# Hybrid decoder trunk on one core: order of the gate normalisations, of a weight cast and of the residual's instructions

## The chip, the cores and the metric

The kernel runs on one core of one Trainium2 chip. The metric is the device time of one execution in microseconds (us). A core has five instruction queues: TensorE (PE), VectorE (DVE), ScalarE (ACT), GpSimd (POOL) and SyncE (SP, which here only starts DMAs). Each engine carries out its own instructions in the order in which they stand; the engines wait for each other by semaphores.

## The reference

Two layers over a sequence of 512 tokens of width 1024, in float32. Cut to what matters here:

```python
n = rmsnorm(h, attn_norm[l])
u, v_sgu, q, k, v_att = split(n @ w_in[l])
u, v_sgu = gelu(u), gelu(v_sgu)
vg = rmsnorm over groups of 128 (v_sgu)              # the "gate values"
y_sgu = u * (tril(w_s) @ vg + b_s)                   # per chunk of 128 tokens
q, k = partial_rope(q), partial_rope(k)
p = softmax(mask(q k^T / 8))                         # 4 heads, two maps each
y_att = rmsnorm((p[0] - lam * p[1]) @ v_att) * (1 - lambda_init)
h = h + concat(y_sgu, y_att) @ w_out[l]
h = h + conv_ffn(rmsnorm(h, ffn_norm[l]))            # gated, causal width 3
```

A last rmsnorm follows the two layers.

## The kernel before, in words

`h` lies transposed in eight SBUF tiles `hT[m]` of 128 features x 512 tokens. Every float32 operand of a product is split into a high part (a cast to float32r) and a low part (what is left), and a product is three matmuls: high x high, high x low, low x high.

**Weights.** `specs` lists blocks of 128x1024 in the order of use; `block(j)` (line 158) starts block j's DMA into `raw`, casts it to `wh` on ACT and subtracts into `wl` on DVE or POOL. There are three buffers each of `raw`, `wh` and `wl`, so a cast waits until PE has done with an older block. In each layer blocks 0 to 19 are `w_in`, 20 to 27 `w_out`, then `w_up` and `w_down`. `AHEAD` says how many blocks past the one in use are prepared; a cast stands in ACT's queue at the place where `block` was called.

**Order.** `pin` chains all instructions of an engine in the order of the code, so the order of the Python calls is the order of each queue (the small rsqrt steps on DVE, lines 378 to 383, alone are free). `run(steps, n)` takes n steps of a generator of projections; after each step one entry of the queue `due` is called: it holds the small work on DVE, ACT and POOL that follows a projection.

**Mixer, layer 0.** `both_first` projects the first half of the gate values (`vs_0`) together with the first queries; then come `vs_1`, the first keys (`k_0`, `k_1`) and the first values (`va`). `gate_values` (line 542) turns a half of gate values into `vg`: gelu and square on ACT, sums, rsqrt and a product on DVE, and `split` (cast on ACT, low part on DVE). `rope` (line 488) turns queries or keys: shuffle and product on DVE, product and sum on POOL, then `split`. The scores are 16 units (4 heads x 4 query tiles, `Unit`): `scores` on PE into two banks, `mn` (mask and minimum) on DVE, `exps` on ACT, `difference` on DVE, the transpose `turn` on PE, `high` and `low`, then `values` on PE. Between these stand up to three steps of the next projections. `spatial` (line 479) masks and splits the 128x128 mixing weights `wsp`.

**Output projection.** `project` fills the banks of output tiles 0 to 3 during the scores; `late` holds tiles 4 and 5; tiles 6 and 7 come last, with blocks 26 and 27. `residual` (line 913) adds a bank to `hT[m]` on DVE, and `norm.feed(m)` makes `gh_f` (ACT), `gl_f` (DVE), the square (ACT) and its sum `acc_f` (POOL). The feed forward part starts with the matmuls `g<-gh_f`.

In the views a helper at line 119 records nearly all instructions, so tiles are read by name; `L119` is no place in the kernel. The number behind a `wh` or `raw` in an order is a buffer's, not a block's.

Of the kernel before, what the change touches and what calls it, by code (L numbers as in the profile page):

```python
# [21 lines left out]
P = 128  # L22
# [4 lines left out]
DEPTH = 2  # L27
# [42 lines left out]
def trunk(ctx: ExitStack, tc, a, out):  # L70
# [16 lines left out]
    def fslot(name):  # L87
        return sp.tile([P, S], F32, tag="s", name=name)
# [53 lines left out]
    specs = []  # L142
# [11 lines left out]
    AHEAD = [2]  # L154

    def block(i):
        while len(loaded) <= min(i + AHEAD[0], len(specs) - 1):
            j = len(loaded)
            n = specs[j].shape[-1]
            if j >= len(specs) - 6:  # L160
                loaded.append(kept(j, n))
                continue
            raw = wp.tile([P, 1024], F32, tag="raw", name=f"raw{j}")[:, :n]
            h = wp.tile([P, 1024], F32R, tag="wh", name=f"wh{j}")[:, :n]
            lo = wp.tile([P, 1024], F32R, tag="wl", name=f"wl{j}")[:, :n]
            (sync if j < 6 else nc.sync).dma_start(out=raw, in_=specs[j])
            act.copy(h, raw)
            mixer = j % (len(specs) // DEPTH) < 28
            eng = gps if (j > 6 if mixer else j % 3 == 1) else dve
            eng.tensor_sub(lo, raw, h.bitcast(F32))  # L170
            loaded.append((h, lo))
        return loaded[i]
# [48 lines left out]
    nxt = [0]  # L221
# [30 lines left out]
    def tok_gemm(banks, xs):  # L252

        for k, x in enumerate(xs):
            if k % 4 == 0:
                h, lo = next_block()
            c = slice(k % 4 * 256, (k % 4 + 1) * 256)
            tok_step(banks, x, (h[:, c], lo[:, c]), k == 0, k == len(xs) - 1)
            yield
# [104 lines left out]
    def rotary_turn():  # L364
        for nm, wide, dst in wides:
            bank = tr_bank(f"rot{nm}")
            for t in range(NT):
                transpose(bank[:, t * P : (t + 1) * P], wide[:, t * P : (t + 1) * P], ident)
            dve.tensor_copy(dst, bank)

    SHUF = [(i + HALF if i < HALF else i - HALF if i < ROT else i) for i in range(32)]

# [58 lines left out]
    def split(name, src, eng=None):  # L431
        h, lo = slot(f"{name}h"), slot(f"{name}l")
        act.copy(h, src)
        (eng or dve).tensor_sub(lo, src, h.bitcast(F32))
        return h, lo
# [10 lines left out]
    for l in range(DEPTH):  # L446
# [28 lines left out]
        def spatial():  # L475
            gps.affine_select(
                out=wsp, in_=wsp, compare_op=ALU.is_ge, fill=0.0, base=0,
                pattern=[[0, NG], [1, P]], channel_multiplier=-1,
            )
            act.copy(ws_h, wsp)  # L480
            gps.tensor_sub(ws_l, wsp, ws_h.bitcast(F32))
# [6 lines left out]
        def rope(banks, store, at, name):  # L488

            t1, sh = [None, None], [None, None]  # L490

            def turn(j):
                sh[j] = tmp(f"{name}{l}_{at + j}sh")
                dve.stream_shuffle(sh[j], banks[j], SHUF)
                t1[j] = tmp(f"{name}{l}_{at + j}t1")
                dve.tensor_mul(t1[j], banks[j], Cr)
                gps.tensor_mul(sh[j], sh[j], Sr)
                gps.tensor_add(t1[j], t1[j], sh[j])

            def part(j):  # L500
                store[at + j] = split(f"{name}{l}_{at + j}", t1[j])

            due.extend([partial(turn, 0), partial(turn, 1), partial(part, 0), partial(part, 1)])

        def query_banks(hp):
            return [mm_bank(f"q{2 * hp + j}_{l}") for j in range(2)]
# [1 line left out]
        def queries(hp):  # L508
            banks = query_banks(hp)
            yield from feat_gemm(banks, xs)  # L510
            rope(banks, qs, 2 * hp, "q")

        def keys(hp):
            banks = [mm_bank(f"k{2 * hp + j}_{l}") for j in range(2)]
            yield from feat_gemm(banks, xs)
            rope(banks, ks, 2 * hp, "k")

        def values(hp):
            banks = [mm_bank(f"va{b}_{hp}_{l}") for b in range(2)]
# [19 lines left out]

        vg, us, ya, ys = [None] * 2, [None] * NG, [None] * NH, [None] * NG  # L540

        def gate_values(gp, banks, steps):

            yield from steps
            gs = sm.tile([P, 8], F32, tag="gs", name=f"gs{l}_{gp}", bufs=2)
            vts, sqs = [None] * 2, [None] * 2
            r = []

            def gelu(b):
                vts[b] = tmp(f"vs{l}_{gp}_{b}")  # L550
                for x in range(2):
                    c = slice(x * 256, x * 256 + 256)
                    t = 2 * b + x
                    act.activation(vts[b][:, c], banks[b][:, c], AF.Gelu_apprx_tanh, scale=norm.rcol[:, t : t + 1])

            def square(b):
                sqs[b] = tmp(f"vq{l}_{gp}_{b}")
                act.activation(sqs[b], vts[b], AF.Square)

            def sums():  # L560
                for b in range(2):
                    dve.reduce_sum(
                        gs[:, 4 * b : 4 * b + 4], sqs[b].rearrange("p (x d) -> p x d", d=P), axis=mybir.AxisListType.X
                    )
                nc.vector.tensor_scalar(gs, gs, 1.0 / P, EPS, op0=ALU.mult, op1=ALU.add)
                r.append(rsqrt(gs, 8, f"gr{l}_{gp}"))

            def normed(b):
                v3 = vts[b].rearrange("p (x d) -> p x d", d=P)
                rb = r[0][:, 4 * b : 4 * b + 4].unsqueeze(2).to_broadcast([P, 4, P])  # L570
                dve.tensor_tensor(out=v3, in0=v3, in1=rb, op=ALU.mult)

            def parts():
                vg[gp] = [split(f"vg{l}_{gp}_{b}", vts[b]) for b in range(2)]

            due.extend([
                partial(gelu, 0), partial(gelu, 1), lambda: (square(0), square(1)), sums, nothing, nothing,
                lambda: (normed(0), normed(1)), parts,
            ])

        def gates(c):

# [154 lines left out]
        def value_banks(gp, bank=mm_bank):  # L737
            return [bank(f"vs{b}_{gp}_{l}") for b in range(2)]

        def both_first():  # L740

            vb, qb = value_banks(0), query_banks(0)

            def steps():
                for k, x in enumerate(xs):
                    tok_step(vb, x, first[0][k], k == 0, k == KD - 1)
                    yield
                    feat_step(qb, x, first[1][k], 0, k == 0, k == KD - 1)
                    yield

            yield from gate_values(0, vb, steps())
            rope(qb, qs, 0, "q")

        def products():
            if l == 0:
                yield from both_first()
                banks = value_banks(1, sc_bank)
            else:
                banks = value_banks(0)
                yield from gate_values(0, banks, tok_gemm(banks, xs))  # L760
                yield from queries(0)
                banks = value_banks(1)
            yield from gate_values(1, banks, tok_gemm(banks, xs))
            yield from keys(0)
            yield from values(0)
            yield from queries(1)
            yield from keys(1)
            yield from values(1)
            yield from gates(0)
            yield from gates(1)  # L770
            yield from project()
# [21 lines left out]
        steps = products()  # L793
        if l == 0:
            run(steps, 16)
            due.extend([nothing] * 4)
            norm.sums()
            for _ in rotary:
                pass
            run(steps, 4)  # L800
            norm.rows()
            run(steps, 2)
            rotary_turn()
        else:
            run(steps, 8)
            due.extend([nothing, nothing])
            run(steps, 2)
            norm.sums()
            run(steps, 3)
            norm.rows()  # L810
            run(steps, 2)
        Cr, Sr = fslot(f"Cr{l}"), fslot(f"Sr{l}")
        dve.tensor_mul(Cr, CT, norm.rstd)
        dve.tensor_mul(Sr, ST, norm.rstd)
        run(steps, 28 - (22 if l == 0 else 15))
        spatial()
        run(steps, 12)
        flush()
        nlam, sgain = small()
# [8 lines left out]
        for i in range(len(todo) + 2):  # L828
# [44 lines left out]
                u2.values()  # L873
            if i in MIX_AT:
                biased.append(mix(MIX_AT.index(i)))
            if i < 8:
                run(steps, 1)
            if i == len(todo):
# [31 lines left out]

        norm = Norm(f"f{l}", C_FN + l * KD)

        def residual(c, banks):
            for j in range(2):
                m = 2 * c + j
                dve.tensor_add(hT[m], banks[j], hT[m])
                norm.feed(m)

        for c in range(2):
            residual(c, pairs[c])  # L920
        run(more)
        residual(2, late)
        banks = [mm_bank(f"wo{6 + j}_{l}") for j in range(2)]
        run(feat_gemm(banks, mixed))
        residual(3, banks)
        pinned[0] = False


# [225 lines left out]
```

## Time and profile before

| | |
|---|---|
| time, median of 3 runs | 1164.84 us (1164.15 to 1165.5) |
| the profiled execution | 1166.31 us, its span 1164.6 us |
| PE busy | 1123.8 us, 96% of the span |
| DVE, ACT, POOL busy | 675.9, 478.3, 395.0 us |
| mean granted PE clock | 0.984 of full speed |
| DMA | 105.24 MB, mean 90 GB/s |

A row of a timeline begins with the start (us from the span's start) and the duration; then engine, line, operation, output<-inputs and shapes; in brackets the idle time of that engine just before, and what released it. A matmul's duration is longer than the step to the next one, since matmuls are pipelined: the step is read from the starts. [...]

### The profile page before, as it was taken

To read this page: it belongs to the slowest core of one execution; us is meant where nothing else is said; L and a number is where in the kernel's file an instruction comes from. 1 tells how busy PE (TensorE), PEld (TensorE's weight loads), DVE (VectorE), ACT (ScalarE), POOL (GpSimd) and SP (SyncE) were. 2 spreads that over 40 slices of the span, in tenths; PEclk is the share of its full clock that TensorE was granted. 3 is DMA by queue.
4 is the path that set the end of the run, shared out by engine and by line. 5 is a ranking of instruction groups with operands and counts; after the bars stand their busy time and mean duration, and the time that the engine had idled before them with its cause. 6 is when DMAs were issued, how large, how long until landed. Compare 5 with 4: busy or idle time off the path is not lost.

```text
span 1164.6 us, 14820 instructions
## 1 busy us (share of the span) xinstructions
PE 1123.8 (96%) x5637; PEld 941.4 (81%) x5637; DVE 675.9 (58%) x1267; ACT 478.3 (41%) x808; POOL 395.0 (34%) x305
## 2 busy tenths in 40 slices
PE   9959999799999999999999999979999999999996
PEld 7957888688888888888899788868888888888886
DVE  6667875475664225764347687735765622565634
ACT  6344453443443224443343554544444412344351
POOL 0446323522241113233456652251333211231351
PEclk9979999899999999999999999989999999999998
DMA  8212112222323223332332211213332232333222
GB/s 265 73 54 73 55 61 76 72 91 92 107 91 108 91 92 95 102 85 88 103 119 75 89 57 54 73 41 114 100 103 96 91 108 92 91 94 105 75 89 73
DMA packets 34215, 105.24 MB, mean 90 GB/s; under 512 B 4064, under 2 KB 8544, under 8 KB 34144
## 3 DMA queue, kind: packets, MB, share of 16 engines
q1 hardware_dynamic: 33712, 104.27, 28.5%
q8 instruction: 44, 0.72, 0.3%
q14 instruction: 27, 0.22, 0.1%
q10 hardware_dynamic: 432, 0.03, 0.0%
HBM read 102.19 MB, written 2.10 MB: 90 GB/s over the span
## 4 chain that ended last, share of the span: by engine, by line
PE 83%; DVE 6%; POOL 4%; ACT 3%; issue 3%; DVEq 0%; POOLq 0%; ACTq 0%
PE g L119 21%; PE v L119 21%; PE dn L119 18%; PE wo L119 6%; PE u L119 4%; PE q L119 3%; PE vs L119 3%; PE dl L119 2%; PE sc L119 1%; POOL wl L119 1%; PE av L119 1%; PE mx L119 1%; ACT wh L119 1%; DVE s L119 1%; DVE hT L119 1%
## 5 line engine op out<-in xcount | busy, mean ns | idle before, releaser
L119 POOL TENSOR_TENSOR wl<-raw,wh 128x1024 fp32r<-128x1024 f32 (+1 forms) x98 | 235.0, 2400 | 584.3 <-ACT wh L119 574.5
L119 ACT CAST wh<-raw 128x1024 fp32r<-128x1024 f32 (+1 forms) x192 | 194.0, 1016 | 373.2 <-issue 189.2
L119 DVE TENSOR_TENSOR wl<-raw,wh 128x1024 fp32r<-128x1024 f32 (+1 forms) x94 | 120.2, 1279 | 129.4 <-ACT wh L119 129.2
L119 PE MATMUL g<-gh_f,wh 128*128 128x512 f32 x352 | 137.1, 390 | 0.0
L119 PE MATMUL v<-gh_f,wh 128*128 128x512 f32 x352 | 137.1, 390 | 0.0
L119 PE MATMUL g<-gh_f,wl 128*128 128x512 f32 x352 | 137.0, 389 | 0.0
L119 PE MATMUL v<-gh_f,wl 128*128 128x512 f32 x352 | 136.9, 389 | 0.0
L119 PE MATMUL g<-gl_f,wh 128*128 128x512 f32 x352 | 136.9, 389 | 0.0
L119 PE MATMUL v<-gl_f,wh 128*128 128x512 f32 x352 | 136.9, 389 | 0.0
L119 DVE SCALAR_TENSOR_TENSOR cv<-up_cv,par,cv 128x512 f32<-128x512 f32 x88 | 74.3, 891 | 7.7 <-ACT cv L119 7.4
L119 PEld LDWEIGHTS g<-gh_f,wl 128*128 128x128 f32 x352 | 66.1, 188 | 13.8
L119 PEld LDWEIGHTS v<-gh_f,wl 128*128 128x128 f32 x352 | 66.1, 188 | 13.7
L119 PEld LDWEIGHTS v<-gh_f,wh 128*128 128x128 f32 x352 | 66.1, 188 | 13.6
L119 PEld LDWEIGHTS g<-gl_f,wh 128*128 128x128 f32 x352 | 66.1, 188 | 13.6
L119 PEld LDWEIGHTS v<-gl_f,wh 128*128 128x128 f32 x352 | 66.1, 188 | 13.6
L119 PEld LDWEIGHTS g<-gh_f,wh 128*128 128x128 f32 x352 | 66.1, 188 | 13.6
L119 DVE SCALAR_TENSOR_TENSOR cg<-up_cg,par,cg 128x512 f32<-128x512 f32 x88 | 71.1, 856 | 6.8 <-ACT cg L119 6.3
L119 DVE TENSOR_TENSOR up_cv<-v,rstd_f 128x512 f32<-128x512 f32 x44 | 30.2, 693 | 67.2 <-PE v L119 67.2
L119 DVE TENSOR_TENSOR up_cg<-g,rstd_f 128x512 f32<-128x512 f32 x44 | 30.0, 692 | 53.7 <-PE g L119 53.4
L119 ACT ACTIVATE s<-s,mn 128x128 f32<-128x128 f32 (+3 forms) x64 | 35.5, 557 | 61.1 <-DVE mn L119 61.1
L119 ACT ACTIVATE cg<-cg 128x512 f32<-128x512 f32 x44 | 27.8, 631 | 46.6 <-DVE cg L119 46.6
L119 DVE TENSOR_TENSOR hT<-dn,hT 128x512 f32<-128x512 f32 x28 | 19.1, 691 | 47.7 <-PE dn L119 47.7
(586 smaller groups left out, 2615.3 us busy)
## 6 DMA issues: line engine op xcount, KB each, us to landing
raw<-in_w_up SPq DMA_DIRECT2D x88, 512.0 KB, 3.4
raw<-in_w_dn SPq DMA_DIRECT2D x40, 512.0 KB, 3.5
raw<-in_w_in SPq DMA_DIRECT2D x36, 512.0 KB, 3.5
raw<-in_w_out SPq DMA_DIRECT2D x16, 512.0 KB, 3.5
hT<-in_xT SPq DMA_DIRECT2D x8, 256.0 KB, 4.7
or<-in_w_in SPq DMA_DIRECT2D x16, 128.0 KB, 4.5
raw<-in_w_dn SPq DMA_DIRECT2D x8, 256.0 KB, 3.4
out<-y SPq DMA_DIRECT2D x8, 256.0 KB, 2.2
```

The costliest lines, as they stand in the source:

```text
L119: return lambda *args, **kw: pin(getattr(self.engine, op)(*args, **kw))
```

## The change

Five edits. (1) In layer 0 the queries' turn is put ahead of the first half's normalisation, and of the second half of gate values only the gelu stays there: squares, sums, rsqrt, products and splits go to a queue `later`, from which each score unit takes two entries; `spatial` is the last of them. (2) In layer 0 the rotary factors `cr` and `sr` are made from the transposed bank directly, and the copies CT and ST (for layer 1) go to ACT. (3) Block 27 (the last of `w_out`) is prepared by a call ahead of the first residual, block 28 after the fourth; `AHEAD` is 0 between. (4) Block 27's low part goes from POOL to DVE. (5) `residual` takes all banks of a group, and each tile's add stands ahead of the `feed` of the tile before it. In layer 1 only (3), (4) and (5) move anything.

```diff
-            mixer = j % (len(specs) // DEPTH) < 28
-            eng = gps if (j > 6 if mixer else j % 3 == 1) else dve
+            i_l = j % (len(specs) // DEPTH)
+            eng = gps if (j > 6 and i_l != 27 if i_l < 28 else j % 3 == 1) else dve
...
-            dve.tensor_copy(dst, bank)
+            turned = fslot(f"{nm}r0")
+            dve.tensor_mul(turned, bank, norm.rstd)
+            act.copy(dst, bank)
+            yield turned
...
+            return [partial(f, b) for f in (gelu, square, sums) for b in range(2)] + [root] + [
+                partial(f, b) for f in (normed, part) for b in range(2)
+            ]
...
-            yield from gate_values(0, vb, steps())
-            rope(qb, qs, 0, "q")
+            yield from steps()
+            g, q = gate_work(0, vb), rope(qb, qs, 0, "q")
+            due.extend([nothing] * 4 + g[:2] + q[:2] + g[2:4] + [lambda: [f() for f in g[4:7]]] + q[2:] + g[7:])
+
+        later = deque()
...
+                yield from tok_gemm(banks, xs)
+                g = gate_work(1, banks)
+                due.extend(g[:2])
+                later.extend(g[2:])
...
-        spatial()
+        if l == 0:
+            later.append(spatial)
+        else:
+            spatial()
...
+            for _ in range(min(2, len(later))):
+                later.popleft()()
             if i < 8:
                 run(steps, 1)
...
-        def residual(c, banks):
-            for j in range(2):
-                m = 2 * c + j
-                dve.tensor_add(hT[m], banks[j], hT[m])
-                norm.feed(m)
-
-        for c in range(2):
-            residual(c, pairs[c])
+        def residual(m0, banks):
+            for m, b in enumerate(banks, m0):
+                dve.tensor_add(hT[m], b, hT[m])
+                if m > m0:
+                    norm.feed(m - 1)
+            norm.feed(m)
+
+        AHEAD[0] = 0
+        block(nxt[0] + 1)
+        residual(0, pairs[0] + pairs[1])
         run(more)
-        residual(2, late)
+        block(nxt[0] + 2)
+        AHEAD[0] = 2
+        residual(4, late)
         banks = [mm_bank(f"wo{6 + j}_{l}") for j in range(2)]
         run(feat_gemm(banks, mixed))
-        residual(3, banks)
+        residual(6, banks)
```

PE's own order is the same in both kernels. ACT at layer 0's residual, before, from the last attention output (`yah`) on:

```order
L119 ACTIVATE yah_3_3_2279<-ot_3_3_2274,sgain_935 128x512
L119 ACTIVATE gh_f_2315<-hT_85,par 128x512
L119 ACTIVATE acc_f_2313<-hT_85 128x512
L119 ACTIVATE gh_f_2321<-hT_86,par 128x512
L119 ACTIVATE sq_f_2325<-hT_86 128x512
...
L119 ACTIVATE gh_f_2359<-hT_90,par 128x512
L119 ACTIVATE sq_f_2363<-hT_90 128x512
L119 CAST wh_2369<-raw_2368 128x1024
L119 CAST wh_2375<-raw_2374 128x1024
L119 CAST wh_2405<-raw_2404 128x1024
```

And there now (`hT_85` to `hT_92` are tiles 0 to 7):

```order
L119 ACTIVATE yah_3_3_2279<-ot_3_3_2274,sgain_902 128x512
L119 CAST wh_2315<-raw_2314 128x1024
L119 ACTIVATE gh_f_2322<-hT_85,par 128x512
L119 ACTIVATE acc_f_2313<-hT_85 128x512
...
L119 ACTIVATE gh_f_2343<-hT_88,par 128x512
L119 ACTIVATE sq_f_2347<-hT_88 128x512
L119 CAST wh_2357<-raw_2356 128x1024
L119 ACTIVATE gh_f_2364<-hT_89,par 128x512
```

Block 27's cast has moved from behind six residual tiles to ahead of the first, block 28's from behind six to behind four.

DVE in layer 0 ahead of the first keys' turn (`gr`, `vs_1`, `vg_1` are the second half of gate values), before:

```order
L383 SCALAR_TENSOR_TENSOR gr_1_830<-gr_1t,gr_1_830 128x8
L119 TENSOR_TENSOR vs_1_0_781<-vs_1_0_781,gr_1_830 128x512
L119 TENSOR_TENSOR vs_1_1_796<-vs_1_1_796,gr_1_830 128x512
L119 TENSOR_TENSOR vg_1_0l<-vs_1_0_781,vg_1_0h 128x512
L119 TENSOR_TENSOR vg_1_1l<-vs_1_1_796,vg_1_1h 128x512
L119 STREAM_SHUFFLE k_0sh<-k_0_666 128x512
L119 TENSOR_TENSOR k_0t_909<-k_0_666,Cr_617 128x512
```

And there now:

```order
L119 TENSOR_TENSOR q_1l<-q_1t_653,q_1h 128x512
L119 TENSOR_TENSOR vs_0_0_587<-vs_0_0_587,gr_0_691 128x512
L119 TENSOR_TENSOR vs_0_1_602<-vs_0_1_602,gr_0_691 128x512
L119 TENSOR_TENSOR vg_0_0l<-vs_0_0_587,vg_0_0h 128x512
L119 TENSOR_TENSOR vg_0_1l<-vs_0_1_602,vg_0_1h 128x512
L119 STREAM_SHUFFLE k_0sh<-k_0_658 128x512
L119 TENSOR_TENSOR k_0t_822<-k_0_658,cr_610 128x512
```

What stands right ahead of the keys is now the first half; the second half has gone behind them.

DVE in score units 2 and 3 of layer 0 (`s_0_2`, `s_0_3` are the maps of head 0, `aTl` the low part of a transposed map), before:

```order
L119 SCALAR_TENSOR_TENSOR s_0_2_0_1051<-s_0_2_1_1052,cf_0_2_1075,s_0_2_0_1051 128x384
L119 TENSOR_TENSOR aTl_0_1_1073<-at_0_1_1061,aTh_0_1_1072 128x256
L119 STREAM_SHUFFLE q_2sh<-q_0_953 128x512
L119 TENSOR_TENSOR q_2t_1099<-q_0_953,Cr_617 128x512
L119 TENSOR_REDUCE o_0_937<-av_0_0_1080 128x128
L119 ISA s_0_3_0_1113,mn_0_3_1112<-sc_0_3_0_1104,mask 128x512
```

And there now:

```order
L386 SCALAR_TENSOR_TENSOR gr_1_1057<-gr_1t,gr_1_1057 128x8
L681 RECIPROCAL cf_0_2_1048<-esum_0_905 128x1
L682 SCALAR_TENSOR_TENSOR cf_0_2_1048<-esum_0_905,cf_0_2_1048,nlam_899 128x1
L119 SCALAR_TENSOR_TENSOR s_0_2_0_1024<-s_0_2_1_1025,cf_0_2_1048,s_0_2_0_1024 128x384
L119 TENSOR_TENSOR aTl_0_1_1046<-at_0_1_1034,aTh_0_1_1045 128x256
L119 TENSOR_TENSOR vs_1_0_790<-vs_1_0_790,gr_1_1057 128x512
L119 STREAM_SHUFFLE q_2sh<-q_0_920 128x512
L119 TENSOR_TENSOR q_2t_1087<-q_0_920,cr_610 128x512
L119 TENSOR_REDUCE o_0_904<-av_0_0_1053 128x128
L119 ISA s_0_3_0_1101,mn_0_3_1100<-sc_0_3_0_1092,mask 128x512
```

The second half's rsqrt steps and its products now stand between the units' instructions.

## Rows read from the trace of the kernel before

**Rows 1.** The page: busy us (share) by engine; DVE's low parts (busy, mean ns).

```profile
PE 1123.8 (96%) x5637; PEld 941.4 (81%) x5637; DVE 675.9 (58%) x1267; ACT 478.3 (41%) x808; POOL 395.0 (34%) x305
...
L119 DVE TENSOR_TENSOR wl<-raw,wh 128x1024 fp32r<-128x1024 f32 (+1 forms) x94 | 120.2, 1279 | 129.4 <-ACT wh L119 129.2
```

**Rows 2.** PE's waits: who waited for whom, total us, times, longest.

```profile
PE sc L119 <- ACT k_0h L119: 11.1, 1, 11.1
PE wo L119 <- ACT wh L119: 9.8, 2, 4.9
```

**Rows 3.** Busy time by stretch: PE, PEld, DVE, ACT, POOL (instructions), PEclk, DMA, GB/s.

```profile
64.57:75.62 11.05, 0.00 (x1) 0.01 (x2) 9.01 (x22) 1.84 (x3) 5.49 (x4) 0.69 0.27 92
77.30:82.20 4.90, 4.90 (x13) 3.80 (x12) 2.49 (x12) 4.33 (x9) 1.72 (x2) 0.50 0.00 2
84.00:107.00 23.00, 22.76 (x121) 17.20 (x120) 16.49 (x46) 10.86 (x29) 12.61 (x7) 1.00 0.23 69
90.00:160.00 70.00, 68.68 (x442) 57.33 (x443) 55.48 (x171) 34.52 (x100) 30.00 (x16) 1.00 0.19 61
```

**Rows 4.** PE's timeline around layer 0's first scores.

```profile
52.67 0.39 PE L119 MATMUL k<-gh_a,wl 128*128 128x512 f32 x1
...
75.62 0.47 PE L119 MATMUL sc<-k_0h,q_0h 64*128 64x128 f32 x2 [11.05 <-ACT k_0h L119]
...
83.97 0.39 PE L119 MATMUL sc<-k_0h,q_0h 64*128 64x256 f32 x2
...
88.99 0.44 PE L119 MATMUL sc<-k_0h,q_0h 64*128 64x384 f32 x2
...
102.94 0.66 PE L119 MATMUL at<-ident,s 128*128 128x128 f32 x4 [0.24 <-DVE aTl L119]
```

**Rows 5.** PE's timeline at the output projection's end, layers 0 and 1.

```profile
203.37 0.39 PE L119 MATMUL wo<-yah,wl 128*128 128x512 f32 x1
...
204.73 0.39 PE L119 MATMUL wo<-yah,wl 128*128 128x512 f32 x1
...
210.17 0.39 PE L119 MATMUL wo<-ys_0h,wl 128*128 128x512 f32 x1
215.44 0.79 PE L119 MATMUL wo<-ys_1h,wh 128*128 128x512 f32 x1 [4.88 <-ACT wh L119]
...
225.23 0.39 PE L119 MATMUL g<-gh_f,wh 128*128 128x512 f32 x1
...
781.45 0.79 PE L119 MATMUL wo<-ys_1h,wh 128*128 128x512 f32 x1 [4.89 <-ACT wh L119]
...
791.52 0.39 PE L119 MATMUL g<-gh_f,wh 128*128 128x512 f32 x1
```

**Rows 6.** ACT's timeline: the first key's cast, and layer 0's residual.

```profile
74.94 0.62 ACT L119 CAST k_0h<-k_0t 128x512 fp32r<-128x512 f32 x1 [4.10 <-POOL k_0t L119]
...
202.49 0.73 ACT L119 ACTIVATE gh_f<-hT,par 128x512 fp32r<-128x512 f32 x1 [4.83 <-DVE hT L119]
203.12 0.61 ACT L119 ACTIVATE acc_f<-hT 128x512 f32<-128x512 f32 x1
...
214.36 2.92 ACT L119 CAST wh<-raw 128x1024 fp32r<-128x1024 f32 x3
```

**Rows 7.** DVE's timeline: normalisations, the first key's turn, the first residual add.

```profile
62.98 1.28 DVE L119 TENSOR_REDUCE gs<-vq 128x4 f32<-128x512 f32 x2 [2.24 <-ACT vq L119]
...
64.50 2.34 DVE L378 TENSOR_SCALAR gr<-gs 128x8 int32<-128x8 int32 x1
...
71.50 0.72 DVE L119 STREAM_SHUFFLE k_0sh<-k 128x512 f32<-128x512 f32 x1
...
201.76 0.69 DVE L119 TENSOR_TENSOR hT<-wo,hT 128x512 f32<-128x512 f32 x1 [3.31 <-PE wo L119]
```

**Rows 8.** POOL's timeline: a weight's low part, and the first key's product.

```profile
64.48 2.34 POOL L119 TENSOR_TENSOR wl<-raw,wh 128x1024 fp32r<-128x1024 f32 x1 [1.03 <-ACT wh L119]
...
72.30 1.27 POOL L119 TENSOR_TENSOR k_0sh<-k_0sh,Sr 128x512 f32<-128x512 f32 x1 [5.48 <-DVE k_0sh L119]
```

More of the change, by code (lines that the diff above doesn't have):

```diff
@@ L501, in part @@
                 store[at + j] = split(f"{name}{l}_{at + j}", t1[j])
-            due.extend([partial(turn, 0), partial(turn, 1), partial(part, 0), partial(part, 1)])
+            return [partial(turn, 0), partial(turn, 1), partial(part, 0), partial(part, 1)]
         def query_banks(hp):
@@ L510, in queries @@
             yield from feat_gemm(banks, xs)
-            rope(banks, qs, 2 * hp, "q")
+            due.extend(rope(banks, qs, 2 * hp, "q"))
         def keys(hp):
@@ L515, in keys @@
             yield from feat_gemm(banks, xs)
-            rope(banks, ks, 2 * hp, "k")
+            due.extend(rope(banks, ks, 2 * hp, "k"))
         def values(hp):
@@ L540, in trunk, with gate_work @@
         vg, us, ya, ys = [None] * 2, [None] * NG, [None] * NH, [None] * NG
-        def gate_values(gp, banks, steps):
-            yield from steps
+        def gate_work(gp, banks):
             gs = sm.tile([P, 8], F32, tag="gs", name=f"gs{l}_{gp}", bufs=2)
-            vts, sqs = [None] * 2, [None] * 2
+            vts, sqs, vg[gp] = [None] * 2, [None] * 2, [None] * 2
             r = []
@@ L558, in square, with sums, root @@
                 act.activation(sqs[b], vts[b], AF.Square)
[L560 to L564, printed above, removed]
+            def sums(b):
+                dve.reduce_sum(
+                    gs[:, 4 * b : 4 * b + 4], sqs[b].rearrange("p (x d) -> p x d", d=P), axis=mybir.AxisListType.X
+                )
+            def root():
                 nc.vector.tensor_scalar(gs, gs, 1.0 / P, EPS, op0=ALU.mult, op1=ALU.add)
@@ L571, in normed, with part, gate_values, of @@
                 dve.tensor_tensor(out=v3, in0=v3, in1=rb, op=ALU.mult)
[L573 to L579, printed above, removed]
+            def part(b):
+                vg[gp][b] = split(f"vg{l}_{gp}_{b}", vts[b])
+            return [partial(f, b) for f in (gelu, square, sums) for b in range(2)] + [root] + [
+                partial(f, b) for f in (normed, part) for b in range(2)
+            ]
+        def gate_values(gp):
+            banks = value_banks(gp)
+            yield from tok_gemm(banks, xs)
+            g = gate_work(gp, banks)
+            def of(*n):
+                return lambda: [g[i]() for i in n]
+            due.extend([of(0), of(1), of(2, 3), of(4, 5, 6), nothing, nothing, of(7, 8), of(9, 10)])
         def gates(c):
@@ L757, in products @@
                 banks = value_banks(1, sc_bank)
-            else:
-                banks = value_banks(0)
-                yield from gate_values(0, banks, tok_gemm(banks, xs))
+                yield from tok_gemm(banks, xs)
+                g = gate_work(1, banks)
+                due.extend(g[:2])
+                later.extend(g[2:])
+            else:
+                yield from gate_values(0)
                 yield from queries(0)
-                banks = value_banks(1)
-            yield from gate_values(1, banks, tok_gemm(banks, xs))
+                yield from gate_values(1)
             yield from keys(0)
@@ L795, in trunk @@
             run(steps, 16)
-            due.extend([nothing] * 4)
             norm.sums()
@@ L802, in trunk @@
             run(steps, 2)
-            rotary_turn()
+            Cr, Sr = rotary_turn()
         else:
@@ L811, in trunk @@
             run(steps, 2)
-        Cr, Sr = fslot(f"Cr{l}"), fslot(f"Sr{l}")
-        dve.tensor_mul(Cr, CT, norm.rstd)
-        dve.tensor_mul(Sr, ST, norm.rstd)
+            Cr, Sr = fslot(f"Cr{l}"), fslot(f"Sr{l}")
+            dve.tensor_mul(Cr, CT, norm.rstd)
+            dve.tensor_mul(Sr, ST, norm.rstd)
         run(steps, 28 - (22 if l == 0 else 15))
-        spatial()
+        if l == 0:
+            later.append(spatial)
+        else:
+            spatial()
         run(steps, 12)
```

## The prediction

> **What bounds the kernel now.** I read the page first: PE is busy for 96% of the span [rows 1], so time is to be won only where PE waits, or where it runs at its lower clock. PE's waits come next, and two of them hold most of the idle time: the first scores wait 11.1 us once for the cast of the first keys, and the output projection waits 4.9 us in each layer for a weight cast on ACT [rows 2]. [...] The timelines say why PE waits. At the scores, DVE spends 62.98 to 71.50 on the second half of gate values and only then turns the first key [rows 7], whose product on POOL, cast on ACT and scores on PE follow within 4.1 us [rows 4, 6, 8]. At the projection, three weight casts stand on ACT behind the residual's tiles and start at 214.36, whereas PE has been ready since 210.56 [rows 5, 6].
>
> **The change part by part.** *Output projection (edits 3 to 5).* 24 matmuls stand between the step that ends block 26 and the first `g<-gh_f`. At the high clock 24 such steps take 210.17 - 204.73 = 5.44 us [rows 5]. In layer 0 the next step would have started at 210.17 + 0.23 = 210.40, and `g` starts at 225.23: 14.83 us, 9.4 too many. In layer 1 PE's last matmul ends at 781.45 - 4.89 = 776.56; less the 0.16 us by which 210.56 lies behind 210.40, that is 776.40, and `g` starts at 791.52: 15.12 us, 9.7 too many [rows 5]. Together 19.1 us are at stake, idle and low clock in one.
>
> Does the cast arrive in time now? It stands first on ACT, but block 23 was kept back for the last two tiles' steps, and its buffer is the one that block 27 takes: the cast waits for the matmul of 203.37 [rows 5]. So it runs from 203.6 to 204.6 (three casts took 2.92 us [rows 6]), its low part on DVE until 205.9 (mean 1.28 us [rows 1]); PE wants both at 210.40. That is safe by 4.5 us. The price is that this new wait stands ahead of the residual on both engines: the first add moves from 201.76 to about 205.9 [rows 7], the first `gh_f` (0.73 us later, as before [rows 6]) to 206.6. From there a tile costs ACT `gh_f` and a square, 0.63 us from start to start plus about 0.55 [rows 6], say 1.2 us; four tiles end at 211.3. Block 28's cast ends at 212.3, POOL's third sum (about 1.3 us, by the row of the same shape [rows 8]) at 212.6, its low part 2.4 us later at 215.0. PE needs that at 215.84 + 0.46 = 216.3. Covered by 1.3 us, which two collisions of POOL and DVE could use up. I take a loss of 0.5 us per layer; its ends are 0 and 3.7 (one more sum and one more weight, 1.3 + 2.4). Tiles 4 to 7 have more: the seventh tile's step of `g` lies 8.2 us behind the first. Gain 18.1 us, from 11.7 to 19.1.
>
> *First scores (edits 1 and 2).* Without a wait PE would begin them at 75.62 - 11.05 = 64.57; unit 1's scores start at 83.97, 19.4 us later. The same work at the high clock is a unit of the form 83.97 to 88.99, 5.0 us, less a transpose and narrower scores, so 4.8 [rows 4]. At stake: 14.6 us.
>
> Now the chain. The queries are turned as soon as the factors exist; what stands before the keys on DVE is the first half's normalisation, and its last cast on ACT stands behind a weight cast that waits until PE has ended the keys' projection, 52.67 + 0.24 = 52.9 [rows 4]. With 1.0 us for that cast, 0.6 for the half's own cast (the 0.62 of `k_0h` [rows 6]) and 0.7 for its low part on DVE, the first key's shuffle starts at 55.2 instead of 71.50. POOL does the block's low part first (53.9 to 56.3), then product and sum, 1.3 us each [rows 8], until 58.9. ACT has block 11's cast in front of `k_0h`; it waits until PE is half through the first values, (52.9 + 64.6) / 2 = 58.7, and ends at 59.7; `k_0h` at 60.3, the low part by 61.5. Should the first half's rsqrt meet POOL twice for 2.3 us, as DVE's step of 64.50 meets POOL's 64.48 [rows 7, 8], a part of which the 52.9 hides, it is 63.6. PE arrives at 64.57: the 11 us are gone in either case, and with them the low clock. What is late next is the other key: POOL has a weight's low part (59.7 to 62.1) between the two keys, so `k_1h` comes at 65.4, and DVE's `mn` of unit 0 stands behind its low part and the small lambda steps, at about 68.4. PE wants the banks back at 64.57 + 4.8 = 69.4.
>
> What was taken from the wait is put into the units. The moved half holds DVE for 71.50 - 62.98 = 8.5 us, 6.3 without its stall on POOL [rows 7]. From 84 to 107 us DVE is busy for 16.49 of 23.0 us [rows 3]: 6.5 us are free, but in pieces, while it waits for scores and exponentials, and PE is already held up for 0.24 us at 102.94 [rows 4]. Placed unit by unit: unit 0's transpose is late by 0.6 us; the rsqrt steps hide behind units 1 and 2; the first product meets POOL's next weight and pushes `mn` of unit 3 so that PE misses its two banks by 2 us; unit 3's transpose and unit 4's banks cost 0.7 each. That makes 4.0 us. Its ends: 0, if all fits into the 6.5 us, and 6.3 plus four collisions of 2.34 us, 15.7, if nothing does. I take 4.0, since most of the pieces do fit. Gain 10.6 us, from -1.1 to 14.6.
>
> The row of 64.50 shows a DVE step of eight columns lasting exactly as long as POOL's 128x1024 beside it. [...]
>
> *The rest.* Two copies leave DVE for ACT and the spatial weights go into unit 4: ACT and POOL are at 41% and 34% [rows 1] and neither stands on the chain there; I cost them at nothing. If that cover were gone they would add a copy, 0.6 us.
>
> *Sum.* 18.1 + 10.6 = 28.7 us off the profiled execution's 1166.31 us: 1137.6. Its span and what lies around it are 1.5 us above the median of the runs, 1164.84; against that, 1136.1 us.
>
> **The rivals.** *Everything fits* (DVE's free 6.5 us take the moved work, no collision delays block 28): 19.1 + 14.6 = 33.7 us, 1131.1. For it: the units' spare time equals the moved work. Against it: DVE follows the units in a fixed order, and PE already waits at 102.94.
>
> *DVE becomes the bound of the units*: 15.7 us are lost there and 18.1 stay, less 1.1: 1147.8. For it the stall at 64.50; against it that POOL idles for up to 5.48 us between its weights [rows 8].
>
> *The projection's wait changes its owner*: block 28's low part comes 3.7 us late in each layer, so 11.7 + 10.6 = 22.3 us: 1142.5. For it the 4.1 us by which the residual starts later; against it the shorter tile.
>
> [...]
>
> **How the numbers follow.** Forecast 0.66 (own range 1132.5 to 1141, from the stalls between half and twice what I took), everything fits 0.14, DVE the bound 0.09, the projection's wait 0.06, slower 0.03, and 0.02 that new waits give nearly all back. The range runs from 1130.5 (a little below the full gain) to 1147, short of the full DVE. A change under 0.2%, 2.3 us, cannot be told from none here: faster 0.95, same 0.02, slower 0.03.
>
> **What would show it.** Right: no wait of PE for `k_0h` or for a `wh` in its waits; PEclk 1.00 through the first scores and both projections' ends; the first `hT` add 4 us later behind the last `wo` of block 23; DVE over 90% busy in units 1 to 4 with PE waiting 1 to 2 us at a time for `mn` or a transposed map. Wrong: a PE gap over 3 us in those units, a PE wait for POOL's `wl` at the first `g`, or a first key later than 64.6.

## The result, and the profile after

The changed kernel takes 1152.7 us (median of 4 runs, 1151.4 to 1155.1) where the kernel before took 1164.7 on the same chip: a ratio of 0.9899, 95% interval 0.9882 to 0.9916. It is faster by 12.0 us, well clear of 0.2%, and lies outside the range of 1130.5 to 1147.0. The direction was right, the size was not: 28.7 us had been forecast. The profiled execution took 1152.52 us with a span of 1150.8, 13.8 less than before. The four executions differ in their mean granted clock, 0.991 in the longest and 0.995 in the shortest, so a difference of a few us between two traces can be the clock's.

PE's waits, the view of [rows 2], after the change (who waited for whom: us in total, times, longest):

```profile
PE ss_f L119 <- DVE acc_f L119: 4.8, 2, 2.4
PE av L119 <- DVE o L119: 3.8, 2, 2.3
PE at L119 <- DVE aTl L119: 3.1, 4, 1.8
PE wo L119 <- DVE hT L119: 3.0, 2, 1.5
PE sc L119 <- DVE mn L119: 1.9, 4, 0.9
...
PE sc L119 <- DVE k_0l L119: 1.7, 2, 0.9
```

Both waits of [rows 2] are gone. What stands there now are waits for DVE, in each place that the change touched. PE's timeline says where, the view of [rows 4, 5]:

```profile
63.79 0.33 PE L119 MATMUL sc<-k_0h,q_0h 64*128 64x128 f32 x2
...
70.30 0.59 PE L119 MATMUL sc<-k_0h,q_0h 64*128 64x256 f32 x2 [0.60 <-DVE mn L119]
73.55 0.30 PE L119 MATMUL at<-ident,s 128*128 128x128 f32 x1 [0.84 <-DVE s L119]
...
87.85 0.36 PE L119 MATMUL av<-va,aTh 128*128 128x256 f32 x1 [1.49 <-DVE o L119]
...
93.77 0.65 PE L119 MATMUL at<-ident,s 128*128 128x128 f32 x4 [1.75 <-DVE aTl L119]
98.16 0.55 PE L119 MATMUL av<-va,aTh 128*128 128x256 f32 x1 [2.35 <-DVE o L119]
...
191.28 0.60 PE L119 MATMUL ot<-ident,o 128*128 128x128 f32 x4
201.54 0.50 PE L119 MATMUL wo<-yah,wh 128*128 128x512 f32 x1 [1.48 <-DVE hT L119]
...
212.59 0.39 PE L119 MATMUL g<-gh_f,wh 128*128 128x512 f32 x1
223.33 0.63 PE L119 MATMUL ss_f<-ident,acc_f 128*128 128x128 f32 x4 [2.42 <-DVE acc_f L119]
228.14 0.40 PE L119 MATMUL v<-gh_f,wh 128*128 128x512 f32 x1
...
775.12 0.39 PE L119 MATMUL g<-gh_f,wh 128*128 128x512 f32 x1
```

The first scores start at 63.79 with no wait for the key's cast. Then six waits follow up to 98.16 (the first is 0.86 us for `k_0l`, at 64.98), one of 1.48 us inside the projection, and one of 2.42 in the middle of the first `g`. Two of the landmarks before, not among its rows so far, from PE's timeline of the kernel before:

```profile
196.34 0.60 PE L119 MATMUL ot<-ident,o 128*128 128x128 f32 x4
...
236.61 0.39 PE L119 MATMUL v<-gh_f,wh 128*128 128x512 f32 x1
```

With these and [rows 5], PE's fixed order lets the 13.8 us be split, each stretch being the difference of two starts:

| stretch of PE's order | before | after | gain | at stake | forecast |
|---|---|---|---|---|---|
| start to layer 0's last `ot` | 196.34 | 191.28 | 5.06 | 14.6 | 10.6 |
| last `ot` to the first `g`, layer 0 | 28.89 | 21.31 | 7.58 | 9.4 | 8.9 |
| first `g` to the first `v`, layer 0 | 11.38 | 15.55 | -4.17 | 0 | 0 |
| first `v` of layer 0 to the first `g` of layer 1 | 554.91 | 546.98 | 7.93 | 9.7 | 9.2 |
| that `g` to the span's end | 373.08 | 375.68 | -2.60 | 0 | 0 |

So 9.5 us of the stake stayed in the scores, 1.8 in each projection up to `g`, and 6.8 were lost newly behind the first `g`, 4.2 in layer 0 and 2.6 in layer 1. DVE shows why. Its timeline after the change, first in the scores, then at layer 0's residual:

```profile
62.72 2.21 DVE L119 TENSOR_TENSOR k_0l<-k_0t,k_0h 128x512 fp32r<-128x512 f32 x1 [1.63 <-ACT k_0h L119]
...
83.39 2.77 DVE L119 TENSOR_TENSOR vs<-vs,gr 128x512 f32<-128x512 f32 x1
...
87.29 0.41 DVE L119 TENSOR_REDUCE o<-av 128x128 f32<-128x256 f32 x1
...
93.64 0.68 DVE L119 TENSOR_TENSOR vs<-vs,gr 128x512 f32<-128x512 f32 x1
...
94.84 2.85 DVE L119 TENSOR_TENSOR q_3l<-q_3t,q_3h 128x512 fp32r<-128x512 f32 x1
97.61 0.41 DVE L119 TENSOR_REDUCE o<-av 128x128 f32<-128x256 f32 x1
...
199.66 1.22 DVE L119 TENSOR_TENSOR wl<-raw,wh 128x1024 fp32r<-128x1024 f32 x1 [6.27 <-ACT wh L119]
200.80 1.28 DVE L119 TENSOR_TENSOR hT<-wo,hT 128x512 f32<-128x512 f32 x2
...
220.35 2.83 DVE L119 TENSOR_TENSOR acc_f<-acc_f,sq_f 128x512 f32<-128x512 f32 x1
```

And POOL's at the same times:

```profile
61.99 2.39 POOL L119 TENSOR_TENSOR wl<-raw,wh 128x1024 fp32r<-128x1024 f32 x1
...
83.22 2.39 POOL L119 TENSOR_TENSOR wl<-raw,wh 128x1024 fp32r<-128x1024 f32 x1 [4.14 <-ACT wh L119]
...
94.37 2.76 POOL L119 TENSOR_TENSOR wl<-raw,wh 128x1024 fp32r<-128x1024 f32 x1 [1.67 <-ACT wh L119]
...
219.76 2.87 POOL L119 TENSOR_TENSOR wl<-raw,wh 128x1024 fp32r<-128x1024 f32 x1 [0.51 <-ACT wh L119]
```

The same product lasts 2.77 us at 83.39 and 0.68 at 93.64. Each of the four long ones starts within a weight's low part on POOL and ends some 0.55 us behind it: 62.72 + 2.21 = 64.93 against 64.38, and likewise 86.16 against 85.61, 97.69 against 97.13, 223.18 against 222.63. What PE waits for (`o`, which empties the bank of `av`; `acc_f`; `k_0l`) is the held instruction or stands soon behind it. `k_0l` took 1.08 us before, and `q_3l` its own time, in the trace of the kernel before:

```profile
102.80 0.68 DVE L119 TENSOR_TENSOR q_3l<-q_3t,q_3h 128x512 fp32r<-128x512 f32 x1
```

One of the waits, 1.75 us for `aTl`, stands behind no such instruction: the long one ahead of it (`s` at 91.49) takes 1.75 us now and took 1.77 before.

DVE's busy time on the page is 697.3 us after and 675.9 before [rows 1], both for 1267 instructions. Two of them are now low parts of 1.2 us that POOL did before; most of the rest is stall, booked as work. The largest piece of it lies at the residual: by groups, the 16 `gl_f` rose from 12.0 to 22.4 us beside POOL's sums and weights.

Behind two of the new waits the clock was low as well. Stretches of the changed kernel, columns as in [rows 3], PEclk being the granted clock as a share of full speed:

```profile
96.00:98.00 2.00, 0.00 (x0) 0.00 (x0) 2.00 (x3) 0.00 (x0) 2.00 (x2) 0.98 0.00 0
98.00:100.00 2.00, 1.84 (x7) 1.78 (x8) 1.14 (x9) 1.68 (x8) 0.18 (x1) 0.50 0.86 256
100.00:102.00 2.00, 2.00 (x8) 1.33 (x8) 1.61 (x4) 1.00 (x2) 0.92 (x1) 0.67 0.02 6
...
223.00:226.00 3.00, 2.67 (x11) 2.20 (x12) 1.94 (x9) 0.00 (x0) 0.00 (x0) 0.70 0.58 175
226.00:230.00 4.00, 4.00 (x18) 3.23 (x17) 1.67 (x7) 1.05 (x1) 0.00 (x0) 0.80 0.02 4
...
785.00:788.00 3.00, 2.15 (x12) 1.88 (x13) 2.05 (x6) 0.00 (x0) 0.26 (x4) 1.00 0.48 158
```

Behind the waits of 2.35 and 2.42 us the granted clock is 0.50 to 0.80 for several us; behind 1.48 us, at 201.54, steps of 0.23 us go on at once. But in layer 1 the same wait for `acc_f` left it at 1.00:

```profile
785.85 0.63 PE L119 MATMUL ss_f<-ident,acc_f 128*128 128x128 f32 x4 [2.40 <-DVE acc_f L119]
```

That is the difference between the 4.2 us lost in layer 0 and the 2.6 in layer 1: the waits are alike, and only one had a low clock behind it.

### The profile page after: what moved, and what is told of

Its sections match the earlier page's. It is cut to its first block, busy times and chain, and to the rows that moved or that the text cites. A ratio compares the mean times of both kernels' runs of the same rounds, so it can differ in the third digit from the quotient of the medians.

```text
span 1150.8 us, 14822 instructions
## 1 busy us (share of the span) xinstructions
PE 1119.3 (97%) x5637; PEld 937.6 (81%) x5637; DVE 697.3 (61%) x1267; ACT 477.4 (41%) x810; POOL 393.0 (34%) x303
## 4 chain that ended last, share of the span: by engine, by line
PE 84%; DVE 7%; ACT 3%; POOL 3%; issue 2%; DVEq 0%; POOLq 0%; ACTq 0%
PE v L119 21%; PE g L119 20%; PE dn L119 18%; PE wo L119 7%; PE u L119 4%; PE vs L119 3%; PE dl L119 3%; PE q L119 2%; PE k L119 1%; ACT wh L119 1%; PE sc L119 1%; PE av L119 1%; PE mx L119 1%; DVE s L119 1%; POOL wl L119 1%
## 5 line engine op out<-in xcount | busy, mean ns | idle before, releaser
L119 POOL TENSOR_TENSOR wl<-raw,wh 128x1024 fp32r<-128x1024 f32 (+1 forms) x96 | 230.1, 2398 | 580.4 <-ACT wh L119 570.5
L119 DVE TENSOR_TENSOR wl<-raw,wh 128x1024 fp32r<-128x1024 f32 (+1 forms) x96 | 123.3, 1284 | 135.9 <-ACT wh L119 135.8
L119 PEld LDWEIGHTS g<-gl_f,wh 128*128 128x128 f32 x352 | 66.5, 189 | 13.8
L119 DVE TENSOR_TENSOR hT<-dn,hT 128x512 f32<-128x512 f32 x28 | 19.1, 690 | 47.8 <-PE dn L119 47.8
```

The lines of the kernel that those rows point to most:

```text
L119: return lambda *args, **kw: pin(getattr(self.engine, op)(*args, **kw))
```

## The experiments

Three causes are held against each other: the banks of tiles 6 and 7, POOL's low parts beside DVE, and plain overload of DVE. Each time is a median with the kernel before beside it on the same chip (1165.1 to 1165.4 us); a ratio is to that kernel, with its 95% interval.

**The projection's edits alone.** Edits 1 and 2 are taken back:

```diff
-            yield from steps()
-            g, q = gate_work(0, vb), rope(qb, qs, 0, "q")
...
+            yield from gate_values(0, vb, steps())
+            rope(qb, qs, 0, "q")
```

> Edits 3 to 5 alone; the first scores are as in the kernel before. Theory (the losses lie stage by stage, as the two traces give them): the projection gains 7.6 us in layer 0 and 7.9 in layer 1 up to the first g, and the wait of the sums' transposes (ss_f) behind it costs 4.2 and 2.6 again, so 8.7 us less than before: 1156.0 us. Rival (the projection gained what was predicted, 18.1 us, and the moved normalisation disturbed it): 1146.6 us and no wait for hT or acc_f on PE.

Measured 1158.69 us, 0.9943 (0.9929 to 0.9956): 6.7 us, 2 less than the theory's, far from the rival's 18.1. Of these 2 us the clock explains most: in this trace it fell behind the wait for `acc_f` in layer 1 too (0.50 from 792 to 794 us), and the first `g` to the first `v` takes 15.57 us there, 13.96 in the changed kernel. Its waits of PE:

```profile
PE sc L119 <- ACT k_0h L119: 11.0, 1, 11.0
PE ss_f L119 <- DVE acc_f L119: 4.9, 2, 2.4
PE wo L119 <- DVE hT L119: 3.0, 2, 1.5
```

The projection loses its us by itself; the moved normalisation has no part in it.

**The four adds first.** From the changed kernel, in both layers:

```diff
+        for m, b in enumerate(pairs[0] + pairs[1]):
+            dve.tensor_add(hT[m], b, hT[m])
         block(nxt[0] + 1)
-        residual(0, pairs[0] + pairs[1])
+        residual(0, pairs[0] + pairs[1], True)
```

> The changed kernel with the four adds of tiles 0 to 3 ahead of block 27's cast and low part. Theory (tiles 6 and 7 take the PSUM banks of tiles 0 and 1, and wait for their adds, which the low part holds up): PE's wait of 1.5 us for hT in each layer is gone, 3.6 us less than the changed kernel, 1149.1 us. Rival (PE only comes earlier to the wait for acc_f, which is DVE's backlog): the wait for acc_f grows from 2.4 to about 4 us and the time stays at 1152.7.

Measured 1147.48 us, 0.9852 (0.9838 to 0.9865). The wait for `hT` is gone. From `ot` to `g` PE now takes 19.50 us in layer 0 (191.66 to 211.16): 28.89 - 19.50 = 9.4, the whole stake. The wait for `acc_f` did not grow, 2.14 us. (The rows account for 3.9 us, the medians show 5.2, within what their intervals allow.) So tiles 6 and 7 did wait for the banks that the first adds empty.

**Block 31's low part on DVE.** It is the one that POOL did at 219.76 beside the last sum, ahead of PE's wait for `acc_f`, 2.42 us in layer 0 and 2.40 in layer 1:

```diff
-            eng = gps if (j > 6 and i_l != 27 if i_l < 28 else j % 3 == 1) else dve
+            eng = gps if (j > 6 and i_l != 27 if i_l < 28 else j % 3 == 1 and i_l != 31) else dve
```

> The changed kernel with block 31's low part on DVE, behind the last acc_f sum, in place of POOL. [...] Rival (DVE is behind because it has 19 us of work without a gap, whatever POOL does): the wait stays above 1.5 us and the time within 1.5 us of 1152.7.

Measured 1146.38 us, 0.9838 (0.9825 to 0.9852): 6.3 us less than the changed kernel. DVE's timeline there:

```profile
217.06 2.45 DVE L119 SCALAR_TENSOR_TENSOR gl_f<-hT,par,gh_f 128x512 fp32r<-128x512 f32 x2
219.43 0.68 DVE L119 TENSOR_TENSOR acc_f<-acc_f,sq_f 128x512 f32<-128x512 f32 x1
220.03 1.21 DVE L119 TENSOR_TENSOR wl<-raw,wh 128x1024 fp32r<-128x1024 f32 x1
```

DVE is as busy in front of the sum as ever; only POOL's low part beside it is gone, and the sum takes 0.68 us. PE waits 0.32. Overload was not the cause of this wait.

**Both of them.**

> Both of the two edits: the four adds ahead of block 27, and block 31's low part on DVE. Theory (two separate causes): the gains add up, 3.6 + 5.5 = 9.1 us, 1143.6 us. Rival (one backlog of DVE behind both waits): no more than the larger of the two alone, 1147 us or above.

Measured 1142.25 us, 0.9805 (0.9792 to 0.9819), 10.5 less than the changed kernel. The gains, 5.2 and 6.3 us, add up within what their intervals allow, so the causes are two. No run shows the 5.5 us of the expected sum; the run with block 31's low part on DVE gave 6.3 in their place. The projection now yields all that was at stake, and what is lost is lost in the scores: `ot` at 191.03, as after the change.

The next runs start from this version. **Three low parts of the score units on DVE** (blocks 11, 14 and 15 are those of 61.99, 83.22 and 94.37):

```diff
-            eng = gps if (j > 6 and
+            eng = gps if (j > 6 and j not in (11, 14, 15) and
```

> From the version with both edits at the projection (1142.25 us, in which the first scores still lose 9.5 of their 14.6 us): in layer 0 the low parts of blocks 11, 14 and 15 on DVE in place of POOL. Theory A (DVE's instructions are stretched by POOL's low parts beside them, k_0l to 2.2 us, the product of vs to 2.8, q_3l to 2.9, and PE's waits for o and aTl come from that): these go back to 0.7 us each, 6 us, against 3.8 us of new work on DVE; PE's two waits for o fall below 1 us each, the clock stays at 1.00, and about 5 us come back: 1137 us. Theory B (DVE simply has too much to do in units 1 to 4, whatever POOL does): 3.8 us more work makes it worse, 1144 to 1146 us.

Measured 1136.91 us, 0.9757 (0.9743 to 0.9770): 5.3 us off by giving DVE 3.8 us more to do. Its DVE timeline:

```profile
81.89 0.68 DVE L119 TENSOR_TENSOR vs<-vs,gr 128x512 f32<-128x512 f32 x1
82.49 1.22 DVE L119 TENSOR_TENSOR wl<-raw,wh 128x1024 fp32r<-128x1024 f32 x1
...
92.42 0.68 DVE L119 TENSOR_TENSOR q_3l<-q_3t,q_3h 128x512 fp32r<-128x512 f32 x1
93.03 0.41 DVE L119 TENSOR_REDUCE o<-av 128x128 f32<-128x256 f32 x1
```

and the stretch around it, with the clock at 1.00 throughout:

```profile
90.00:105.00 15.00, 13.47 (x93) 11.51 (x94) 12.76 (x36) 6.73 (x19) 7.78 (x6) 1.00 0.23 65
```

The held instructions are back at 0.68, the waits for `o` fell from 3.8 to 0.8 us in all, and `ot` comes at 185.83. This is what tells POOL's hold from the load: by load alone it had to become slower. Two things the rows add. Of the 5.2 us by which `ot` is earlier, 1.5 are there at the first transpose already (72.05, 73.56 without the edit): with block 11's low part off POOL's queue the second key's product no longer stands behind it. That is POOL's order, not its hold on DVE. And the wait for `aTl` stays, 1.77 us; with fewer or none of the moved steps in these units (the next run, and the one without the second half's work) it is 0.24 and 0.29. That one belongs to the load. In the expectations that follow, "port" is only a name for theory A; why POOL's low part holds these instructions, no run shows.

**One step of the second half a unit, not two.**

```diff
-            for _ in range(min(2, len(later))):
+            if later:
                 later.popleft()()
...
-            later.append(spatial)
+            later.insert(7, spatial)
```

> From the same version: one step of the second half's work at the end of each unit in place of two, so that it lies in units 0 to 9, not 0 to 4 (the spatial weights stand eighth, in unit 7). Theory A (collisions with POOL's low parts): the stretched instructions are others, as it falls; within 2.5 us of 1142.25. Theory B (units 1 to 4 are overfilled): half the work leaves them, two thirds of the 9.5 us come back, 1136 us.

Measured 1138.83 us, 0.9771 (0.9758 to 0.9785): 3.4 us, between the two. The rows are not clean either: the waits for `o` are gone, but a product of 2.62 us (101.00) and a small step of 2.05 (111.40) are now the held ones, with waits of 1.6 and 1.5 us. By itself it does not decide between the two.

**The product on ACT.**

```diff
+                if l == 0 and gp == 1:
+                    for x in range(4):
+                        c = slice(x * P, x * P + P)
+                        act.activation(vts[b][:, c], vts[b][:, c], AF.Identity, scale=r[0][:, 4 * b + x : 4 * b + x + 1])
+                    return
                 dve.tensor_tensor(out=v3, in0=v3, in1=rb, op=ALU.mult)
```

> From the same version: the second half's product with its factors as four scaled copies of 128 columns on ACT for each bank, in place of DVE's one of 512. Theory A (port): the product of 2.8 us is gone from the place ahead of the first o, PE's wait of 1.5 us for o at the first 512-wide unit is gone and the later ones shrink, but q_3l is still held up: 3 us less, 1139.3 us. Theory B: 1.4 us of DVE's work is gone, 1.4 us less, 1140.8 us; the wait for the first o stays above 1 us.

Measured 1139.60 us, 0.9780 (0.9766 to 0.9793). The wait for the first `o` is gone, as theory A has it, but a wait of 3.29 us for `aTl` at 93.50 has taken its and the others' place. No hold by POOL makes it: `q_3l` takes 0.68 us here, and DVE itself is idle for 2.03 us ahead of `q_2l`, whose product on POOL stands in the queue behind block 14's low part (84.49 to 86.91). That the time is A's 1139.3 is luck; A expected `q_3l` to be held.

**Without the second half's work.**

```diff
-                later.extend(g[2:])
+                later.append(lambda: vg.__setitem__(1, vg[0]))
```

> From the same version: squares, sums, root, product and parts of layer 0's second half of gate values are left out (the first half's parts stand in their place), so its output is not the reference's; POOL's work and the other orders stay. It prices the moved work. Theory A and B alike: the 9.5 us are what the moved work costs, 1132.8 us; the difference is in the rows: by A, q_3l is still stretched beside POOL's low part and 2 to 3 us of waits stay, 1135 us; by B nothing stays. Rival C (the moved work is not the cause, the later arrival of the first keys' low part and of the second key is): 1139 us or more.

Measured 1135.08 us, 0.9743 (0.9730 to 0.9756). `ot` comes at 184.91, so the moved work cost 191.03 - 184.91 = 6.1 of the 9.5 us. The other 3.4 are not its doing, as rival C had it for all of them: in units 0 and 1 PE still waits for `k_0l` (0.88), `mn` (0.60) and `s` (1.17), 2.7 us of them. The time is theory A's, its reason not: `q_3l` is no longer held (0.67 us), since it now runs at 91.35, ahead of block 15's low part at 92.09.

**Combinations.** The low parts on DVE with the slower pace, with the product on ACT, and with both:

> The version with the three low parts on DVE (1136.91 us) and, with it, one step of the second half's work a unit. Theory (port first, then order): PE's wait of 1.8 us for aTl stands behind a unit with the moved product and q_3l and shrinks; the waits of 1.6 and 1.5 us that the slower pace had at 111 and 115 us come in; 1135 to 1138 us. Rival (the two cures act on separate losses and add up, 5.3 + 3.4 us): 1133.5 us.

> The three low parts on DVE and the second half's product on ACT. Theory (both cure the same collision of the product with block 14's low part): of the product's 2.7 us only its 0.7 us of DVE's own time are still to be had, twice: 1135.5 us. Rival (they add up): 1134.3 us.

> All three: low parts of blocks 11, 14, 15 on DVE, one step a unit, the product on ACT. Theory: 1134.5 us, near the 1135.1 us of the version without the second half's work at all, since little of the moved work is then left before PE; rival (the later waits at 111 and 115 us stay): 1137 us.

Measured 1135.93 us, 0.9749 (0.9735 to 0.9762); 1136.87, 0.9756 (0.9743 to 0.9769); 1135.90, 0.9749 (0.9736 to 0.9763). The cures do not add up, and the product on ACT gives nothing once its collision is gone. With the first, `ot` comes at 184.83, as early as without the second half at all (where the three low parts were still on POOL). It is the version to keep: 29.1 us below the kernel before. What still waits there is seen at 112.19:

```profile
108.69 0.55 PE L119 MATMUL at<-ident,s 128*128 128x128 f32 x3 [1.72 <-DVE aTl L119]
112.19 0.36 PE L119 MATMUL av<-va,aTh 128*128 128x256 f32 x1 [1.53 <-DVE or_3t L384]
```

**Edit 4 undone**, from the changed kernel:

```diff
-            eng = gps if (j > 6 and i_l != 27 if i_l < 28 else j % 3 == 1) else dve
+            eng = gps if (j > 6 if i_l < 28 else j % 3 == 1) else dve
```

> The changed kernel with edit 4 undone: block 27's low part on POOL as before, so that the adds of tiles 0 to 3 stand first on DVE though the cast is still first on ACT. Theory (DVE's low part, not the cast, holds back the adds that free the banks of tiles 6 and 7): PE's wait of 1.5 us for hT is gone in both layers, as with the adds placed first, and block 27's low part is in time (about 202 us against 206): 1147.5 to 1150 us, the wait for acc_f staying above 2 us. Rival (the cast or the residual's own order holds PE): the wait for hT stays and the time is 1152.7 us or more.

Measured 1151.16 us, 0.9882 (0.9865 to 0.9900), not the 1147.5 to 1150 expected. The wait for `hT` is gone in both layers, so it was DVE's low part that held the adds. But PE now waits longer for `acc_f`, and DVE's first `gl_f` is held beside POOL's 2.40 us of 200.30:

```profile
PE ss_f L119 <- DVE acc_f L119: 6.9, 2, 3.4
```

```profile
200.88 2.37 DVE L119 SCALAR_TENSOR_TENSOR gl_f<-hT,par,gh_f 128x512 fp32r<-128x512 f32 x1 [2.15 <-ACT gh_f L119]
```

From `ot` to `g` it takes the full-stake 19.50 us, from `g` to `v` 17.62 where the changed kernel takes 15.55: 1.8 won, 2.1 lost in layer 0. Part of that loss is the clock's and not the order's: this trace is of an execution of 1155.38 us, well above the median, and in it the clock fell to 0.50 behind the wait in both layers, in the changed kernel's trace only in layer 0. The medians, with overlapping intervals, tell no difference from the changed kernel. A PE that comes earlier, to a DVE held once more, waits longer further on.

## Why the prediction was wrong in size

*The stakes were right.* 19.1 us in the projections: run by run, 7.6 + 7.9 - 6.8 = 8.7 were there at once, and two small edits brought 10.5 more. Of the scores' 14.6, the version with low parts and pace has 196.34 - 184.83 = 11.5.

*The projection's loss of 0.5 us a layer is the step that failed.* It measured 1.8 + 4.2 = 6.0 us in layer 0 and 1.8 + 2.6 = 4.4 in layer 1, beyond even the upper end of 3.7. The casts and times were right: block 27's cast was forecast for 203.6 and the first add for 205.9; with PE 5.06 us earlier that is 198.5 and 200.8, and the rows have 198.52 and 200.80. ACT's row:

```profile
198.52 1.05 ACT L119 CAST wh<-raw 128x1024 fp32r<-128x1024 f32 x1 [5.91 <-PE wo L119]
```

But the question asked of those 4.1 us of delay was only when block 28's low part would be ready. That was in time; PE never waits for it. Two other readers of the same delay were not asked: tiles 6 and 7, which take the PSUM banks that the first adds empty, and the end of the chain, the last sum, which shared its time with POOL's next weight. The prediction counted what PE reads and left out what PE must find empty.

*The scores' stalls of 4.0 us are the other mis-sized term*: 9.5. The first key came in time (its cast ended at 62.7, where 60.3 was counted, and the 11 us are gone), but its low part, forecast for 61.5 and for 63.6 at the latest, was held and ended at 64.93, and PE waited 0.86 us for it. The collision of the first product with a weight was right. What was not priced: `q_3l` and `k_0l`, two instructions which the change only shifted in time onto POOL's low parts, and the low clock behind a wait of 2.35 us. The second key was forecast for 65.4 and came at 68.1: the weight between the keys ran on POOL from 61.99, 2.3 us later than forecast, and the key's product behind it took 1.73 us where 1.3 was counted. By the run without the second half's work, 6.1 of the 9.5 us are the moved work's and 3.4 are not. The bound of four collisions named the right mechanism; the value was taken too near its lower end.

*What the row of 64.50 showed decided most of it.* Four DVE instructions, each with two inputs in SBUF, were held by POOL's low parts, as the four pairs of rows show, with 2.2 to 2.9 us where 0.68 is the instruction's own. Not every DVE instruction beside POOL was: the two sums `gs` at 77.00 take 0.64 us each within POOL's low part of 76.68, and two `hT` adds at 207.63, which read one bank and one tile, take 0.64 each beside POOL's sums. The step of 64.50 that the prediction points to has one input in SBUF. That it was held is clear, since the same step takes 0.17 us at 79.14, with POOL idle. What decides which DVE instructions are held, no row shows.

*The rivals.* "DVE becomes the bound" put all the loss into the units, 15.7 us; they lost 9.5. "The projection's wait changes its owner" was right in kind, but named the wrong owner and too small a price, 3.7 us a layer against 6.0 and 4.4. The low clock came for a few us behind some of the waits (0.50 and 0.67 from 98 to 102 us in the changed kernel), not as a lasting state.

*The signs.* DVE was busy for 25.1 of the 27 us from 71 to 98, as forecast; the clock of 1.00 through scores and projections was not. None of the three signs of being wrong came: the longest gap of PE in the units was 2.35 us against 3, PE waited for no `wl` of POOL, and the first key was there before 64.6. They watched the price of single gaps and the places that had been thought of; the time was lost in several shorter waits and in another place.

## What to carry to other kernels

When a wait is taken away by putting work ahead of other work, list for each delayed instruction everything that waits for it: its data's readers, those who need the buffer or bank that it empties, and the last link of a chain of sums. Look for DVE instructions that come to lie beside a long POOL instruction, also among those that only shift in time; a row several times as long as its twin shows one that is held (here 2.77 us against 0.68), and the busy share hides it. Here such stalls were cured by moving POOL's work to the held engine, though that engine was the busier one (61% of the span against 34%): 6.3 us with one low part, 5.3 with three. When two traces of one change differ by a few us, compare the clock behind each wait before giving the difference a cause.

## What the runs showed of the hardware

A DVE instruction held by POOL is booked as long, not as idle: the page has 21.4 us more busy time for as many instructions, of which the two low parts new on DVE explain 2.4. The price ran both ways in two of the four pairs: POOL's low part took 2.76 and 2.87 us beside `q_3l` and `acc_f`, where 2.39 is its own; beside `k_0l` and the product at 83.39 it took 2.39.

The length of a wait did not tell what PE's clock did behind it. It stayed at 1.00 behind the two waits of 1.48 us in the changed kernel. Behind 2.14 to 2.42 us it fell in some places and not in others: in the changed kernel behind 2.42 us in layer 0 and not behind 2.40 in layer 1; with the four adds first behind 2.14 us in layer 0 and not behind 2.14 in layer 1. The wait of 2.35 us in the scores lowered it in the changed kernel, and not in the trace with block 31's low part on DVE. In the trace with low parts, pace and product together it was at 0.50 from 115 to 118 us, behind waits of only 1.06 and 0.29 us. A stretch of each of the last two, columns as in [rows 3]:

```profile
98.00:100.00 2.00, 1.64 (x10) 1.54 (x11) 1.13 (x8) 1.49 (x7) 0.37 (x1) 1.00 0.75 219
```

```profile
116.00:118.00 2.00, 2.00 (x9) 1.60 (x8) 2.00 (x4) 1.74 (x4) 1.86 (x2) 0.50 0.00 0
```

What decides it, these runs leave open. Its price is shown: a wait of 2.42 us cost 4.2 us where the clock fell, one of 2.40 cost 2.6 where it did not.
